# One fp32 product per chunk for two Gram matrices of a gated DeltaNet head

## The chip, the cores and the metric

The kernel runs on one core of one Trainium2 chip. The metric is the device time of one execution, in microseconds (us). Three runs of the kernel before gave 2437.64, 2440.42 and 2441.45 us; the median is 2440.42 us. One more execution was profiled; it took 2440.88 us, and the span of its trace is 2439.1 us. All rows below come from that execution.

## What is computed

The program is two decoder layers on a sequence of 1024 tokens with 1024 channels. Layer 0 mixes tokens with a gated DeltaNet of 8 heads of 128 channels, layer 1 with a causal convolution module; after each comes a squared-ReLU MLP. Only the DeltaNet matters here. Cut to what the change touches, it computes

```python
q, k, v = split(silu(causal_conv(h @ w_in)))          # q and k are then normalised per token
decay = exp(where(causal, gam[:, None] - gam[None, :], -inf))
a_kk  = where(strict, einsum('cd,sd->cs', k * beta, k) * decay, 0)   # first Gram matrix
t_inv = solve(eye + a_kk, eye)
a_qk  = einsum('cd,sd->cs', q, k) * decay                            # second Gram matrix
# scan over chunks: v_new = u - w @ state; o = q_dec @ state + a_qk @ v_new; state = ...
```

Both Gram matrices of a chunk have the keys as one operand. They are taken in fp32.

## The kernel before, in words

The sequence is cut into two halves of 512 tokens (`hf`), and a half into four chunks of 128 (`NC2`). A head of one half is a unit `u`, 0 to 15 (`u = 8*hf + h`). Keys, queries and values lie with channels on the partitions and 512 tokens side by side.

Three engines, TensorE, VectorE (DVE) and ScalarE (ACT), run in an order that is written out by hand. Each job is a generator; `add` gives each of its steps a due time, and at the end all steps are emitted in order of due time. Within these three engines instructions run in that order. GpSimdE (POOL) and the DMA queue of SyncE (SP) are ordered by the framework. Due times are in stages: unit `u` is projected in stage `u` or a little earlier, prepared from `u + 1` on (`head_prep`, times `PREP_AT`), its 16x16 diagonal blocks are inverted on GpSimdE (`head_sub`, at `u + 1 + 0.298`), the whole block by TensorE in stage `u + 2` (`head_inv`, first step at 0.0574, its first matmul at 0.2093), and the scan over the chunks runs in stage `u + 3` (`head_scan`, 24 steps from -0.063 to 0.8984; its matmuls on the state L632 and L645 to L649, its update of the state L655). `head_decay` makes E, the exponentials of the decay, at `u + 0.6769` to `u + 1.1256`.

What fills TensorE are the dense projections: each tile is 24 passes of 512 columns (L229 to L231), eight steps of three. `PLAN` says how many tiles a stage holds: projection tiles, tiles of the output gate z, and tiles of the output product; a stage without an entry has three projection tiles and, from stage 12 on, one z tile, which comes first. The tiles of a stage share it evenly: with n tiles, one lasts 1/n of a stage, and its eight steps are spread over that. Stage 7 has one tile more, for the gates of the second half; it comes first. After that tile, the gates pass through a chain of small steps (`token_gates`, times `G1_AT` after the tile's end; the reciprocal L354 and the GpSimdE steps L355 to L364 at 0.487, the matmuls L369 and L370 on `gcol` at 0.7341, exponentials on ScalarE at 0.7578). The weights of the next tile are split in two during a tile: `whi` on ScalarE at 0.4696 of the tile, `wlo` on VectorE (L396) at 0.6631.

`conv` takes a projected tile out of PSUM (ScalarE, L415 and L420, 0.04 after the tile's end), adds three taps on VectorE (L423), and applies SiLU (ScalarE, L426) at 0.3287 after the tile's end.

The 13 steps of `head_prep`, with their due times after `u + 1`, are: transposes of k (-0.0922); squares of it with their sums, and the addition of an epsilon on GpSimdE (-0.0063); the matmuls of the first Gram matrix, L483 (0.0109); the norms (0.0442); NT, the masked first matrix, L493, and the two DMAs that bring its diagonal blocks to GpSimdE's layout (0.1551); the scaled copies kd, L503 (0.1822); transposes of q (0.2501), squares of it (0.4031); transposes of v (0.7425) and their scaling (0.7828); the matmuls of the second Gram matrix, L526 (0.8401); its product with E, L528 (0.9083); q times its decay (1.542). Two PSUM banks, tag `pp`, serve all of it. Keys and queries have four buffers each.

Of the kernel before, what the change touches and what calls it, by code (L numbers as in the profile page):

```python
# [11 lines left out]
AF = mybir.ActivationFunctionType  # L12
ALU = mybir.AluOpType
# [7 lines left out]
HALF = 512  # L21
NH = 8
NCH = S // P
NC2 = NCH // 2
# [15 lines left out]
W_HI = 0.4696  # L40
W_LO = 0.6631
CONV_AT = (0.04, 0.0952, 0.1701, 0.2145, 0.3287)
PREP_AT = (-0.0922, -0.0063, 0.0109, 0.0442, 0.1551, 0.1822, 0.2501, 0.4031, 0.7425, 0.7828, 0.8401, 0.9083, 1.542)
DECAY_AT = (0.6769, 0.9619, 1.1256)
SUB_AT = 0.298
INV_AT = (
# [19 lines left out]
H0_AT = (0.8992, 1.98, 2.4218, 2.6956, 3.874, 4.2736, 6.2935, 6.8047)  # L66
G1_AT = (-0.0095, 0.088, 0.1601, 0.2135, 0.3241, 0.487, 0.7341, 0.7578, 1.2185, 1.3557)
PLAN = {
    0: (3, 0, ()), 1: (1, 4, ()), 2: (1, 2, ()), 3: (0, 2, ()), 4: (3, 0, ()), 5: (3, 0, ()), 7: (4, 0, ()), 8:
    (4, 0, ()), 14: (2, 1, ()), 15: (2, 1, ()), 16: (0, 2, ()), 17: (0, 2, (3,)), 18: (0, 0, (6, 0, 4, 7, 1)),  # L70
}


# [51 lines left out]
def tile_hybrid(ctx, tc, xT, c, adaT, cols, rows, gates, w_gate, w_first, w_dn, w_dno, w_cf, w_cfo,  # L125
                w_1, w_2, consts, out):
    nc = tc.nc
    ve, sc, te, gp = nc.vector, nc.scalar, nc.tensor, nc.gpsimd
    uid = [0]

    def nm(s):
        uid[0] += 1
        return f"{s}_{uid[0]}"
# [31 lines left out]
    def bank(tag):  # L165
        return banks["pool"].tile([P, HALF], F32, name=nm(tag), tag=tag, bufs=banks[tag])
# [3 lines left out]
    def blk(j):  # L170
        return slice(j * P, (j + 1) * P)
# [78 lines left out]
    def power(o, i, e):  # L250
        gp.tensor_tensor(o, i, expo[e][:, 0:i.shape[1]], op=ALU.pow)
# [49 lines left out]
        gp.memset(expo[e], e)  # L301


    db = Bufs("dn", pre=2, k=4, q=4, v=2, NT=2, A=2, Xc=2, o=2, gb=2, Rt=2, vt=2)
    VC = [P, NC2, P]
    GS = [P, NH, NC2]
    future = dp("future", P)
# [7 lines left out]
    beta, gam, negam, kdec, gdr = {}, {}, {}, {}, {}  # L315

    def v3(t):
        return t.rearrange("p (c m) -> p c m", m=P)

    def bc_col(t2d):  # L320
        return t2d.unsqueeze(2).broadcast_to(VC)
# [88 lines left out]
    def conv(d, nt, hf, tag, out):  # L410

        ps = d["ps"]
        pre = db("pre", HALF + CONV - 1)
        gp.tensor_copy(pre[:, 0:CONV - 1], hist[:, nt, :])
        sc.copy(pre[:, CONV - 1:], ps)  # L415
        if hf == 0:
            gp.tensor_copy(hist[:, nt, :], pre[:, HALF:])
        a = db(tag)
        b_ = C_CONV + nt * CONV
        sc.activation(a, ps, AF.Copy, scale=col[:, b_ + 3:b_ + 4])  # L420
        yield
        for j in range(3):
            ve.scalar_tensor_tensor(a, pre[:, j:j + HALF], col[:, b_ + j:b_ + j + 1], a,  # L423
                                    op0=ALU.mult, op1=ALU.add)
            yield
        sc.activation(a, a, AF.Silu)  # L426
        out[tag] = a
        yield
# [12 lines left out]
    def temp(kind, u):  # L441

        i = {"V": u % 2, "kd": 2 + u % 3, "E": 5 + u % 3}[kind]
        return hb(f"ax{i}_{1 if u < 10 else 0}")
# [19 lines left out]
    def head_prep(u, d):  # L464

        hf, h = divmod(u, NH)
        k = d["k"]

        kd = temp("kd", u)
        ssk, ssq = sm("ssk", NC2), sm("ssq", NC2)  # L470

        ps = bank("pp")
        for j in range(NC2):
            te.transpose(ps[:, blk(j)], k[:, blk(j)], ident)
        yield
        for j in range(NC2):
            sc.activation(kd[:, blk(j)], ps[:, blk(j)], AF.Square, accum_out=ssk[:, j:j + 1])
        gp.tensor_scalar(ssk, ssk, L2_EPS, None, op0=ALU.add)
        yield

        g = bank("pp")
        for j in range(NC2):
            te.matmul(g[:, blk(j)], lhsT=k[:, blk(j)], rhs=k[:, blk(j)], start=True, stop=True)  # L483
        yield
        nk = sm("nk", NC2)
        power(nk, ssk, 0.5)
        br2 = d["br2"] = sm("br2", NC2)
        ve.reciprocal(br2, ssk)
        ve.tensor_mul(br2, br2, beta[hf][:, h, :])
        yield  # L490
        NT = d["NT"] = db("NT")
        for j in range(NC2):
            ve.scalar_tensor_tensor(NT[:, blk(j)], g[:, blk(j)], br2[:, j:j + 1], d["E"][:, blk(j)],  # L493
                                    op0=ALU.mult, op1=ALU.mult)

        pitch = 8 * (NB * P + NB)
        d_in = dr.tile([NC2, pitch], F32, name=nm("d_in"), tag="d_in", bufs=2)
        nc.sync.dma_start(bass.AP(d_in.tensor, d_in.offset, [[P, P], [pitch, NC2], [1, P]]), v3(NT))
        A = d["A"] = db("A", [NB, NB], p=32)
        nc.sync.dma_start(A, bass.AP(d_in.tensor, d_in.offset, [[NB * P + NB, 32], [P, NB], [1, NB]]))  # L500
        yield
        for j in range(NC2):
            sc.activation(kd[:, blk(j)], ps[:, blk(j)], AF.Copy, scale=kdec[hf][:, h, j:j + 1])  # L503
        d["kd"] = kd
        yield
        ps = bank("pp")
        for j in range(NC2):
            te.transpose(ps[:, blk(j)], d["q"][:, blk(j)], ident)
        yield
        for j in range(NC2):  # L510
            sc.activation(ps[:, blk(j)], ps[:, blk(j)], AF.Square, accum_out=ssq[:, j:j + 1])
        gp.tensor_scalar(ssq, ssq, L2_EPS, None, op0=ALU.add)
        yield
        vn = hb("lo")
        ps = bank("pp")
        for j in range(NC2):
            te.transpose(ps[:, blk(j)], d["v"][:, blk(j)], ident)
        yield
        ve.tensor_tensor(v3(vn), v3(ps), bc_col(nk), op=ALU.mult)
        d["vn"] = vn  # L520
        eq = d["eq"] = sm("eq", NC2)
        ve.tensor_scalar(eq, ssq, RMS_EPS * P, None, op0=ALU.mult)
        yield
        g = bank("pp")
        for j in range(NC2):
            te.matmul(g[:, blk(j)], lhsT=k[:, blk(j)], rhs=d["q"][:, blk(j)], start=True, stop=True)  # L526
        yield
        ve.tensor_tensor(d["E"], g, d["E"], op=ALU.mult)  # L528
        d["kq"] = d["E"]
        yield  # L530

        ve.tensor_tensor(d["q"], d["q"], d["gb"], op=ALU.mult)
        d["qs"] = d["q"]
        yield
# [21 lines left out]
    def head_inv(u, d):  # L556

        NT = d["NT"]
        V, VT, W = temp("V", u), db("VT"), db("W")
# [16 lines left out]
        def at(t, j, r, c, n):  # L576
            return t[r:r + n, j * P + c:j * P + c + n]
# [3 lines left out]
        for j in range(NC2):  # L581
            te.matmul(ps[:, blk(j)], lhsT=NT[:, blk(j)], rhs=VT[:, blk(j)], start=True, stop=True)  # L582
        yield
# [9 lines left out]
        for b_, n in ((32, P), (64, 64)):  # L593
            yield from transposed(n)
            w = bank("pi")
            for j in range(NC2):
                for r in range(0, P, 2 * b_):
                    te.matmul(at(w, j, r + b_, r, b_), lhsT=at(NT, j, r, r + b_, b_), rhs=at(VT, j, r, r, b_),
                              start=True, stop=True)
# [163 lines left out]
    for u in range(2 * NH):  # L763
        n = f"{u // 8}{u % 8}"
        add("prep" + n, head_decay(u, heads[u]), *[max(u + p_, 0.98 + p_ / 100) for p_ in DECAY_AT])
        add("prep" + n, head_prep(u, heads[u]), *[u + 1 + p_ for p_ in PREP_AT])
        add("inv" + n, head_sub(u, heads[u]), u + 1 + SUB_AT)
# [488 lines left out]
```

## Time and profile before

| | |
|---|---|
| median of three runs | 2440.42 us (2437.64 to 2441.45) |
| the profiled execution, its time and its span | 2440.88 us, 2439.1 us |
| TensorE (PE) busy | 2378.8 us, 98% |
| VectorE (DVE) busy | 1724.6 us, 71% |
| ScalarE (ACT) busy | 1102.5 us, 45% |
| GpSimdE (POOL) busy | 419.5 us, 17% |
| chain that ended last, share of TensorE | 84% |

PE is TensorE's matmuls, PEld its weight loads, which run beside them. The stretch up to about 700 us holds the DeltaNet half of the work. In rows of the time order, the first number is the start in us after the span's start, the second the length; a bracket at the end gives how long the engine stood idle before the instruction and what released it. Matmuls overlap in the pipeline, so their spacing is read from one start to the next.

### The profile page before, as it was taken

Reading aid. Unit: us, or ns where it says so; the run is one execution under the profiler, and the core shown is the slowest. Engines: PE = TensorE matmul, PEld = TensorE weight load, DVE = VectorE, ACT = ScalarE, POOL = GpSimd, SP = SyncE. Lnnn points to the kernel's source line nnn. Section 1 sums busy time; section 2 is a strip of 40 time slices with the busy share of each in tenths; the row PEclk is TensorE's granted clock in tenths of the full one; section 3 lists DMA queues with packets and bytes.
Section 4 is the critical chain, followed back from the end, with each engine's and each line's share of the span. In section 5 each row is a group of like instructions: output and inputs, shape, how many; then the busy total and the mean of one; then the engine's idle time right before and its main releaser. Section 6 shows DMA issues by size and latency. Waiting matters only on the chain.

```text
span 2439.1 us, 31861 instructions
## 1 busy us (share of the span) xinstructions
PE 2378.8 (98%) x11962; PEld 1967.7 (81%) x11962; DVE 1724.6 (71%) x2634; ACT 1102.5 (45%) x1934; POOL 419.5 (17%) x903
## 2 busy tenths in 40 slices
PE   7889999999999999999999999999999999999998
PEld 6678888888777888888888888878888888888887
DVE  6656777676688664555899998899888766443447
ACT  4666776664346323333633334553333345333323
POOL 0546556455411000000000001100000001000003
PEclk9999999999999999999999999999999999999999
DMA  7342232333645654443223222323233232223223
GB/s 291 107 136 82 74 91 78 99 92 106 202 157 171 207 181 142 150 141 104 95 98 101 95 95 96 104 87 104 95 97 101 92 125 90 100 97 102 96 95 130
DMA packets 117994, 286.98 MB, mean 118 GB/s; under 512 B 35024, under 2 KB 44496, under 8 KB 117840
## 3 DMA queue, kind: packets, MB, share of 16 engines
q1 hardware_dynamic: 117840, 284.95, 36.0%
q8 instruction: 94, 1.54, 0.3%
q14 instruction: 60, 0.49, 0.1%
HBM read 275.40 MB, written 9.50 MB: 117 GB/s over the span
## 4 chain that ended last, share of the span: by engine, by line
PE 84%; DVE 7%; POOL 4%; DMA 3%; issue 1%; ACT 1%; SPq 0%; DVEq 0%; POOLq 0%; ACTq 0%
PE pd L229 25%; PE pd L231 25%; PE pd L230 25%; POOL X L546 1%; PE pp L943 1%; DVE wlo L396 1%; POOL T L544 1%; DMA raw<-in_adaT_dram 1%; DVE tl L994 1%; DVE tl L992 1%; DVE lo L241 1%; DVE raw L203 1%; DVE ax L254 1%; PE pi L582 1%; PE ps L645 1%
## 5 line engine op out<-in xcount | busy, mean ns | idle before, releaser
L229 PE MATMUL pd<-hh,whi 128*128 128x512 f32 x2016 | 820.0, 407 | 22.4 <-ACT whi L220 12.8
L231 PE MATMUL pd<-hh,wlo 128*128 128x512 f32 x2016 | 790.8, 393 | 2.3 <-DVE wlo L396 2.3
L230 PE MATMUL pd<-lo,whi 128*128 128x512 f32 x2016 | 789.6, 392 | 0.5 <-DVE lo L241 0.5
L393 ACT CAST whi<-raw 128x1024 fp32r<-128x1024 f32 x382 | 398.7, 1044 | 543.0 <-PE pd L230 518.0
L396 DVE TENSOR_TENSOR wlo<-raw,whi 128x1024 fp32r<-128x1024 f32 x382 | 466.9, 1223 | 19.5 <-ACT whi L393 17.8
L229 PEld LDWEIGHTS pd<-hh,whi 128*128 128x128 f32 x2016 | 381.6, 189 | 92.6 <-ACT whi L220 12.8
L231 PEld LDWEIGHTS pd<-hh,wlo 128*128 128x128 f32 x2016 | 380.3, 189 | 86.4 <-DVE wlo L396 4.0
L230 PEld LDWEIGHTS pd<-lo,whi 128*128 128x128 f32 x2016 | 382.1, 190 | 69.1 <-DVE lo L241 1.7
L229 PE MATMUL pd<-xh,whi 128*128 128x512 f32 (+1 forms) x1056 | 405.1, 384 | 1.3 <-DVE ax L254 1.3
L230 PE MATMUL pd<-xl,whi 128*128 128x512 f32 (+1 forms) x1056 | 404.1, 383 | 0.3 <-DVE xl L241 0.3
L231 PE MATMUL pd<-xh,wlo 128*128 128x512 f32 (+1 forms) x1056 | 404.1, 383 | 0.0
L922 DVE SCALAR_TENSOR_TENSOR cv<-u,col,cv 128x512 f32<-128x512 f32 x480 | 358.4, 748 | 9.6 <-ACT cv L918 1.8
L254 DVE SCALAR_TENSOR_TENSOR ax<-pd,mod,ax 128x512 f32<-128x512 f32 x280 | 207.8, 746 | 165.8 <-PE pd L231 164.8
L241 DVE TENSOR_TENSOR xl<-ts,xh 128x512 fp32r<-128x512 f32 x128 | 88.3, 690 | 245.8 <-ACT ts L866 245.3
L860 ACT ACTIVATE tz<-pd 128x512 f32<-128x512 f32 x128 | 76.5, 598 | 392.9 <-PE pd L231 392.9
L229 PEld LDWEIGHTS pd<-xh,whi 128*128 128x128 f32 x1056 | 198.5, 188 | 40.7 <-DVE ax L254 1.1
L230 PEld LDWEIGHTS pd<-xl,whi 128*128 128x128 f32 x1056 | 198.5, 188 | 39.1 <-DVE xl L241 0.5
L231 PEld LDWEIGHTS pd<-xh,wlo 128*128 128x128 f32 x1056 | 198.4, 188 | 38.8
L203 DVE CUSTOM_DVE_ANT_0 raw<-raw,condb 128x1024 f32<-128x1024 f32 x96 | 117.3, 1222 | 36.8 <-DMA raw<-in_adaT_dram 36.4
L952 POOL TENSOR_SCALAR lnst<-mv 128x1 f32<-128x1 f32 x32 | 16.2, 506 | 530.7 <-DVE mv L951 360.7
L546 POOL TENSOR_TENSOR X<-X,T 32x15 f32<-32x15 f32 (+7 forms) x240 | 98.0, 408 | 18.7
L544 POOL TENSOR_TENSOR T<-X,A 32x15 f32<-32x15 f32 (+7 forms) x240 | 84.1, 350 | 27.2 <-DMA A<-d_in 9.4
(215 smaller groups left out, 2246.1 us busy)
## 6 DMA issues: line engine op xcount, KB each, us to landing
raw<-in_w_dram SPq DMA_DIRECT2D x260, 512.0 KB, 3.6
raw<-in_adaT_dram SPq DMA_DIRECT2D x96, 512.0 KB, 3.9
raw<-in_w_dn_dram SPq DMA_DIRECT2D x57, 512.0 KB, 4.0
raw<-in_w_cf_dram SPq DMA_DIRECT2D x32, 512.0 KB, 3.8
raw<-in_w_dno_dram SPq DMA_DIRECT2D x16, 512.0 KB, 3.7
raw<-in_w_cfo_dram SPq DMA_DIRECT2D x16, 512.0 KB, 3.7
tz<-in_xT_dram SPq DMA_DIRECT2D x16, 256.0 KB, 7.8
raw<-in_w_first_dram SPq DMA_DIRECT2D x8, 512.0 KB
```

The source lines that it names most:

```text
L203: ve.tensor_tensor_reduce(out=raw, in0=raw, in1=condb, op0=ALU.mult, op1=ALU.add, scale=1.0, scalar=0.0, accum_out=mod[l][j][:, k:k + 1])
L229: te.matmul(ps, lhsT=w[0][:, s_], rhs=ah, start=(first and i == 0), stop=False)
L230: te.matmul(ps, lhsT=w[0][:, s_], rhs=al, start=False, stop=False)
L231: te.matmul(ps, lhsT=w[1][:, s_], rhs=ah, start=False, stop=(last and i == n - 1))
L241: ve.tensor_tensor(lo, x32, hi.bitcast(F32), op=ALU.subtract)
L254: ve.scalar_tensor_tensor(AX[hf][k], ps, g[:, k:k + 1], AX[hf][k], op0=ALU.mult, op1=ALU.add)
L393: sc.copy(hi, raw)
L396: ve.tensor_tensor(lo, raw, hi.bitcast(F32), op=ALU.subtract)
L544: gp.tensor_tensor(t, X[:, 0:i + 1, i:i + 1].broadcast_to(sh), A[:, i:i + 1, i + 1:].broadcast_to(sh), op=ALU.mult)
L546: gp.tensor_tensor(X[:, 0:i + 1, i + 1:], X[:, 0:i + 1, i + 1:], t, op=ALU.subtract)
L860: sc.activation(r, d[0], AF.Relu)
L922: ve.scalar_tensor_tensor(cv, u[:, j:j + HALF], col[:, b_ + j:b_ + j + 1], cv, op0=ALU.mult, op1=ALU.add)
```

## The change

Keys and queries of a unit become the two halves of one tile (`pair`), so that one matmul with a chunk's keys as weights and 256 columns, the chunk's keys and then its queries, gives both Gram matrices. Two chunks fill a PSUM bank; `gram(0)` and `gram(1)` fill two. The copies kd move ahead of the matmuls, the norms too; the product of the second matrix with E becomes two instructions and moves up behind NT and its DMAs. Due times are changed accordingly: 11 steps, the norms at 0.0442, the two Gram steps at 0.085 and 0.11, NT and the product with E at 0.1551, the rest as before. Keys and queries have four paired buffers. Four entries of `PLAN` go: stages 7 and 8 have three projection tiles in place of four (stage 7 with the gate tile besides), and stages 14 and 15 have three in place of two, with one z tile as before.

```diff
-PREP_AT = (-0.0922, -0.0063, 0.0109, 0.0442, 0.1551, 0.1822, 0.2501, 0.4031, 0.7425, 0.7828, 0.8401, 0.9083, 1.542)
+PREP_AT = (-0.0922, -0.0063, 0.0442, 0.085, 0.11, 0.1551, 0.2501, 0.4031, 0.7425, 0.7828, 1.542)
...
-    0: (3, 0, ()), 1: (1, 4, ()), 2: (1, 2, ()), 3: (0, 2, ()), 4: (3, 0, ()), 5: (3, 0, ()), 7: (4, 0, ()), 8:
-    (4, 0, ()), 14: (2, 1, ()), 15: (2, 1, ()), 16: (0, 2, ()), 17: (0, 2, (3,)), 18: (0, 0, (6, 0, 4, 7, 1)),
+    0: (3, 0, ()), 1: (1, 4, ()), 2: (1, 2, ()), 3: (0, 2, ()), 4: (3, 0, ()), 5: (3, 0, ()), 16: (0, 2, ()), 17: (0, 2, (3,)), 18: (0, 0, (6, 0, 4, 7, 1)),
...
-    db = Bufs("dn", pre=2, k=4, q=4, v=2, NT=2, A=2, Xc=2, o=2, gb=2, Rt=2, vt=2)
+    db = Bufs("dn", pre=2, kq=4, v=2, NT=2, A=2, Xc=2, o=2, gb=2, Rt=2, vt=2)
...
-        a = db(tag)
+        if tag == "v":
+            a = db(tag)
+        else:
+
+            if "pair" not in out:
+                out["pair"] = db("kq", [2, HALF])
+            a = out["pair"][:, 0 if tag == "k" else 1]
...
-        yield
-
-        g = bank("pp")
         for j in range(NC2):
-            te.matmul(g[:, blk(j)], lhsT=k[:, blk(j)], rhs=k[:, blk(j)], start=True, stop=True)
-        yield
+            sc.activation(kd[:, blk(j)], ps[:, blk(j)], AF.Copy, scale=kdec[hf][:, h, j:j + 1])
+        d["kd"] = kd
+        yield
+
+
+        def gram(i):
+            g = bank("pp").rearrange("p (c t m) -> p c t m", c=2, t=2)
+            for j in range(2):
+                c_ = blk(i * 2 + j)
+                te.matmul(g[:, j], lhsT=k[:, c_], rhs=d["pair"][:, :, c_], start=True, stop=True)
+            return g
+
...
+        g = [gram(0)]
+        yield
+        g.append(gram(1))
+        yield
         NT = d["NT"] = db("NT")
         for j in range(NC2):
-            ve.scalar_tensor_tensor(NT[:, blk(j)], g[:, blk(j)], br2[:, j:j + 1], d["E"][:, blk(j)],
+            ve.scalar_tensor_tensor(NT[:, blk(j)], g[j // 2][:, j % 2, 0], br2[:, j:j + 1], d["E"][:, blk(j)],
...
-        yield
-        for j in range(NC2):
-            sc.activation(kd[:, blk(j)], ps[:, blk(j)], AF.Copy, scale=kdec[hf][:, h, j:j + 1])
-        d["kd"] = kd
+        E = v3(d["E"])
+        for i in range(2):
+            ve.tensor_tensor(E[:, i * 2:i * 2 + 2], g[i][:, :, 1], E[:, i * 2:i * 2 + 2], op=ALU.mult)
+        d["kq"] = d["E"]
...
-        yield
-        g = bank("pp")
-        for j in range(NC2):
-            te.matmul(g[:, blk(j)], lhsT=k[:, blk(j)], rhs=d["q"][:, blk(j)], start=True, stop=True)
-        yield
-        ve.tensor_tensor(d["E"], g, d["E"], op=ALU.mult)
-        d["kq"] = d["E"]
```

## Rows read from the trace of the kernel before

**Rows 1.** The page's first part: an engine's busy time, share of span, instructions.

```profile
PE 2378.8 (98%) x11962; PEld 1967.7 (81%) x11962; DVE 1724.6 (71%) x2634; ACT 1102.5 (45%) x1934; POOL 419.5 (17%) x903
```

**Rows 2.** What TensorE waited for, 0 to 900 us: total, times, longest.

```profile
PE pp L369 <- POOL gcol L364: 5.3, 2, 4.0
PE ps L645 <- DVE vt L641: 4.9, 3, 2.3
PE pi L582 <- DVE VT L562: 4.4, 1, 4.4
```

**Rows 3.** TensorE's groups, whole span, shapes apart: weights, columns; busy us, mean ns; idle.

```profile
L483 PE MATMUL pp<-k 128*128 128x128 f32 x128 | 16.8, 274 | 0.0
L979 PE MATMUL pp<-ident,lnst 128*8 128x128 f32 x8 | 2.2, 272 | 4.7 <-POOL lnst L954 4.7
L369 PE MATMUL pp<-gcol,kcl 128*128 128x32 f32 x4 | 0.8, 286 | 5.3 <-POOL gcol L364 5.3
```

**Rows 4.** TensorE in order of time: head 0's first Gram matrix; then 256-column passes.

```profile
91.55 1.05 PE L483 MATMUL pp<-k 128*128 128x128 f32 x8
...
92.68 0.39 PE L230 MATMUL pd<-lo,whi 128*128 128x512 f32 x1
92.91 0.40 PE L231 MATMUL pd<-hh,wlo 128*128 128x512 f32 x1
...
2411.00 0.28 PE L229 MATMUL pd<-xh,whi 128*128 128x256 f32 x1
2411.12 0.28 PE L230 MATMUL pd<-xl,whi 128*128 128x256 f32 x1
```

**Rows 5.** Groups of VectorE and ScalarE, 0 to 900 us.

```profile
L528 DVE TENSOR_TENSOR ax<-pp,ax 128x512 f32<-128x512 f32 x16 | 11.0, 685 | 7.7 <-PE pp L526 7.7
L503 ACT ACTIVATE ax<-pp,kdec 128x128 f32<-128x128 f32 x64 | 18.1, 363 | 0.0
```

**Rows 6.** ScalarE, VectorE and TensorE in order of time, start of stage 12.

```profile
444.32 0.63 ACT L457 ACTIVATE ax<-ax 128x512 f32<-128x512 f32 x1
445.38 1.12 ACT L503 ACTIVATE ax<-pp,kdec 128x128 f32<-128x128 f32 x4
...
444.98 1.13 DVE L493 SCALAR_TENSOR_TENSOR NT<-pp,br,ax 128x128 f32<-128x128 f32 x4 [0.64 <-ACT ax L457]
...
447.82 0.34 DVE L655 SCALAR_TENSOR_TENSOR S<-S,gl,ps 128x128 f32<-128x128 f32 x1
...
449.29 0.39 PE L632 MATMUL ps<-S,k 128*128 128x128 f32 x2
```

**Rows 7.** Head 0: E's exponential, NT, and TensorE's wait for its inverse.

```profile
95.34 0.63 ACT L457 ACTIVATE ax<-ax 128x512 f32<-128x512 f32 x1
...
96.30 1.12 DVE L493 SCALAR_TENSOR_TENSOR NT<-pp,br,ax 128x128 f32<-128x128 f32 x4
...
130.99 1.47 PE L582 MATMUL pi<-VT,NT 128*128 128x128 f32 x8 [4.43 <-DVE VT L562]
```

**Rows 8.** Stage 7: the gate chain on GpSimdE, and TensorE's wait for its end.

```profile
300.30 0.29 POOL L352 TENSOR_SCALAR gz<-gy 128x32 f32<-128x32 f32 x1
...
312.94 0.24 POOL L364 TENSOR_TENSOR gcol<-gq,nea 128x32 f32<-128x32 f32 x1
...
313.23 0.41 PE L369 MATMUL pp<-gcol,kcl 128*128 128x32 f32 x2 [1.25 <-POOL gcol L364]
```

**Rows 9.** Busy us of PE, PEld, DVE, ACT, POOL; granted clock; DMA share, GB/s.

```profile
120.00:140.00 20.00, 15.57 (x78) 12.99 (x77) 12.70 (x26) 12.52 (x31) 6.38 (x15) 0.91 0.61 188
300.00:320.00 20.00, 18.57 (x112) 14.64 (x111) 13.23 (x28) 13.74 (x33) 12.06 (x36) 1.00 0.34 99
```

**Rows 10.** Stages 16 and 17: ScalarE and TensorE in order of time.

```profile
571.93 0.70 ACT L420 ACTIVATE v<-pd,col 128x512 f32<-128x512 f32 x1
...
572.79 0.38 PE L638 MATMUL ps<-Rt,ax 128*128 128x128 f32 x2
...
601.81 0.49 PE L645 MATMUL ps<-vt,ax 128*128 128x128 f32 x2 [2.35 <-DVE vt L641]
```

More of the change, by code (lines that the diff above doesn't have):

```diff
@@ L478, in head_prep @@
         gp.tensor_scalar(ssk, ssk, L2_EPS, None, op0=ALU.add)
+        for j in range(NC2):
+            sc.activation(kd[:, blk(j)], ps[:, blk(j)], AF.Copy, scale=kdec[hf][:, h, j:j + 1])
+        d["kd"] = kd
         yield
-        g = bank("pp")
-        for j in range(NC2):
-            te.matmul(g[:, blk(j)], lhsT=k[:, blk(j)], rhs=k[:, blk(j)], start=True, stop=True)
-        yield
+        def gram(i):
[4 more added lines that the diff above has]
+            return g
         nk = sm("nk", NC2)
@@ L522, in head_prep @@
         ve.tensor_scalar(eq, ssq, RMS_EPS * P, None, op0=ALU.mult)
-        yield
-        g = bank("pp")
-        for j in range(NC2):
-            te.matmul(g[:, blk(j)], lhsT=k[:, blk(j)], rhs=d["q"][:, blk(j)], start=True, stop=True)
-        yield
-        ve.tensor_tensor(d["E"], g, d["E"], op=ALU.mult)
-        d["kq"] = d["E"]
         yield
```

## The prediction, made before the change was run

> **What bounds the kernel now.** The page first: TensorE is busy 98% of the span [rows 1], so the time changes only if TensorE gets less work, or if it stands still more or less than today. Next, the waits of TensorE in the stretch that holds the DeltaNet half (0 to 900 us): they are few, and each has a place [rows 2]. In the stages 1 to 16 that the change touches they are the two waits for the gate columns (L369, 5.3 us in all; the second, in stage 7, is 1.25 us [rows 8]), one wait of 4.4 us for head 0's inverse (L582), and 4.9 us in three waits of the scan (L645). Steady stages have practically none: there VectorE, ScalarE, GpSimdE and the SP queue run beside TensorE with some slack. So I price TensorE's own instructions first, and then ask at each boundary whether a moved step uses up that slack.
>
> **TensorE's instructions.** An fp32 product is two instructions here (L483: 128 for 64 products [rows 3]). Eight of them, head 0's first Gram matrix, take from 91.55 to 92.68 less the one 512-column pass in between (0.23): 0.90 us, 0.1125 each [rows 4]. Both matrices of a head: 16 halves, 1.80 us. After the change: 8 halves of 256 columns. No row shows an fp32 half of more than 128 columns, so two bounds. Lower: it streams one column per cycle as the 256-column fp32r pass does, 0.12 us [rows 4]; 0.96 us a head, 13.4 us saved over 16 heads. Upper: two cycles a column, as a 512-column pass, 0.23 us [rows 4]; 1.84 us a head, +0.6 us in all. What sets today's 0.1125, the columns or the weight load? L979 moves 128 columns against 8 weight columns and takes 272 ns, as long as L483 with 128 (274): columns. L369 moves 32 columns against 128 weight columns and takes 286: weights too [rows 3]. Both sides cost the same in a square product, so halving the loads saves nothing unless columns are cheaper than L979 says. I take the upper bound, **+0.6 us**; VectorE and SP cannot hide it either way.
>
> The Trainium skill (TensorE: Matmul & The Clock Gate, "LDWEIGHTS (loading the stationary operand)") has a weight load cost its columns at 1.2 GHz, an estimate of 107 ns for 128: by that rule alone the load would be today's limit and the lower bound would come within reach. Its page FP8 and Floating Point Precision ("TensorE Precision Notes") counts four passes for true fp32, which over two instructions is the upper bound. No row separates them; the first is the first rival below.
>
> **Work that is merely moved.** Four scaled copies of kd (L503, 363 ns each [rows 5], 1.1 us) go from behind the exponentials of E to ahead of them on ScalarE. At the boundary of stage 12, E's exponential is done at 444.95 and VectorE's first NT step starts at 444.98 [rows 6]: there ScalarE is the later one, so NT moves by 1.1 us. Behind NT come the two new products with E; today's single one is 685 ns [rows 5], so two halves cost between 0.7 and 1.4 us; I take 0.85. What is queued behind on VectorE (taps of the convolution, wlo, the state update L655) comes 1.9 us later. The state update ended at 448.16 and TensorE took it up at 449.29 [rows 6]: 1.1 us of slack, plus 0.9 because TensorE now does the second Gram matrix before that point. It just holds: cost nought, and if it does not, some 0.3 us at each such head. The d_in transfer behind NT shifts SP's queue by the same 1.1 us, and weight loads behind it are issued about a tile before use, which covers that. Gram matrices now hold both pp banks until the products with E are done; q's transposes come at slot 0.2501, three us after NT's slot: hidden. The pair buffer waits for the scan of head u-4, which ends at u-0.10, half a stage ahead of k's copy at u+0.37: hidden. The product with E, and its matmul, vanish from slots 0.84 and 0.91: nobody was held there.
>
> **Early stages.** Head 0's NT starts at 96.30, E's exponential ends at 95.97 [rows 7]: with 1.1 us more, NT moves by 0.8, and so does the chain through d_in, substitution and d_out to the 4.43 us wait at 130.99. But TensorE meanwhile does head 1's second matrix inside that wait (0.9 us that it need not do later). Net -0.1; where W of the inverse (behind the new products) comes late, up to +1.0. I take **+0.3**.
>
> **The plan: stage 7.** Stages 7 and 8 lose a tile each, 14 and 15 gain one. Work is conserved, but the gate columns are a chain on GpSimdE. It ends at 313.18, after the substitution of head 6 is done (300.30) and 26 small steps; TensorE waited from 311.98 [rows 8]. In the new plan the gate tile ends at 7.25 instead of 7.2, so L369 lands at slot 7.984: TensorE has one tile less to do ahead of it (24 passes of 0.23, 5.5 us) and two more of the last tile's eight steps (1.4 us): it arrives at about 307.7. GpSimdE's chain starts about 1 us earlier, since one wlo step (1.2 us) leaves the place before NT; it ends near 312.1. The wait grows from 1.25 to 4.4: **+3.1 us** (bounds +1 and +5). A 4.43 us wait at 131 went with a granted clock of 0.91 over its 20 us, that is 1.2 GHz for 3.6 of them; the 1.25 us wait did not (1.00) [rows 9]. At half speed 3.6 us do the work of 1.8: **+1.7 us**. Head 7's first product of both matrices also waits, for q's SiLU (below), but within that slow stretch: nought more.
>
> **The new wait on q.** Until now the matrix with q ran at u+1.84. Now TensorE needs q at u+1.085, in order, so all projections queue behind it. In a stage with four tiles q is the third; its SiLU stands at u+1.0787. At heads 12 to 14 TensorE has three tile steps and one scan product (2.3 us) before it, which covers copies and SiLU: **+0.5 us** for all such boundaries together (0 to 1.5). At head 15 stage 16 has only two long tiles: one tile step, L638 (572.79 today, 0.9 earlier without the old matrix), then the product, at 572.1. ScalarE's copy of v ends at 572.63 [rows 10]; add 1.1 for kd, and q's SiLU, now behind that copy rather than ahead of it: 573.75. A wait of 1.65 us. The next wait, the 2.3 us one [rows 2] near 601, hangs on head 15's own chain and is shortened by what TensorE lost; that chain moves by 1. Net **+0.5** (-1 to +3).
>
> **Sum.** 0.6 + 0.3 + 3.1 + 1.7 + 0.5 + 0.5 = 6.7 us on the profiled execution of 2440.88 us (span 2439.1): 2447.6. The median of the three runs is 0.46 below it, so 2447.1; I say 2447.
>
> **Rivals.** (1) Columns are cheap (the lower bound): 14 us less than my sum, 2433, faster. For it: L369's 286 ns; against: L979's 272. It decides as soon as a 256-column half takes under 0.16 us. Chance 0.15. (2) The waits are hidden: GpSimdE begins the gate chain before it finishes other steps, and q is ready: only +0.6 remains, 2441. For it: in the substitution GpSimdE already lets other small steps in; against: 26 serial steps cannot be shortened. Chance 0.25. (3) Stage 8, one tile shorter, no longer covers head 7's substitution, and TensorE also waits for its inverse in stage 9, 3 us and another spell at 1.2 GHz: 2452. Against: NT to the inverse has about 6 us of room. Chance 0.08. The forecast itself, 0.52.
>
> **How the numbers follow.** A measurement of this kernel tells 0.2% (4.9 us) from no change. Of the forecast's 0.52, three quarters lie beyond +4.9 (0.39), with rival 3: slower 0.47. The other quarter and rival 2: same 0.38. Rival 1: faster 0.15. Range: 2436 to 2454; it leaves out rival 1 and a tail above, and takes in the bounds of the stage 7 wait and of the tail.
>
> **What would show it.** L483's successors: a mean pitch of 0.23 (or 0.12). TensorE's wait for gcol in stage 7: over 4 us, with a clock below 1.00 in those 20 us. A wait of about 1.7 us for q's SiLU at stage 16. NT a microsecond later than today in stages after a three-tile stage, and no wait at L632 from it. If the gate wait stays near 1 us, the step on the plan is wrong; if TensorE's busy time falls by over 10 us, the step on columns is.

## The result and the profile after

The changed kernel takes 2458.53 us (median of 4 runs, 2456.39 to 2459.39) against 2440.44 for the kernel before beside it (4 runs): a ratio of 1.0075, 95% interval 1.0057 to 1.0092. It is 18 us slower. The forecast, 2447, had the direction; the time lies above the range (2436 to 2454). The profiled execution took 2456.39 us with a span of 2454.6, 15.5 us more than the span before.

The page's first line for TensorE, to set beside [rows 1]:

```profile
PE 2384.2 (97%) x11834; PEld 1967.4 (80%) x11834; DVE 1726.7 (70%) x2650; ACT 1106.7 (45%) x1936; POOL 421.2 (17%) x903
```

There are 128 instructions fewer on TensorE and 5.4 us more busy time. The projections are the same and the Gram products take no longer (below), so I looked at the waits and at the granted clock next. First TensorE's waits in the changed kernel between 290 and 400 us (total, times, longest):

```profile
PE ps L654 <- DVE vt L650: 4.5, 1, 4.5
PE pp L368 <- POOL gcol L363: 4.1, 1, 4.1
PE pi L597 <- DVE W L593: 0.6, 1, 0.6
PE pp L494 <- ACT kq L431: 0.3, 1, 0.3
```

That is 9.5 us; before, the same stretch held the gate wait of 1.3 [rows 2, 8] and 0.2 more. (vt is a short step on VectorE between two products of the scan, W one between two products of the inverse.) Then stretches of 20 us (busy us of TensorE, its instructions, granted clock, DMA share, GB/s), three of the changed kernel and two of the kernel before:

```profile
300.00:320.00 20.00, 15.63 (x76) 0.83 0.33 99
340.00:360.00 20.00, 15.52 (x89) 0.92 0.27 74
360.00:380.00 20.00, 20.00 (x141) 0.91 0.19 56
...
340.00:360.00 20.00, 20.00 (x127) 1.00 0.30 88
360.00:380.00 20.00, 20.00 (x157) 1.00 0.29 77
```

Before, all three stood at 1.00 (the first is in [rows 9]). The clock has two levels here, 2.4 and 1.2 GHz, and the figure is its mean over the stretch. What the clock takes is read straight from this: 20 x (1 - 0.83) = 3.4 us in the first, 20 x (0.08 + 0.09) = 3.4 in the other two. So 290 to 400 us alone holds 8.0 us of new waits and 6.8 of clock, 14.8 of the 15.5 us. The rest of the kernel nearly balances: from 100 to 290 us TensorE waits 1.5 us longer, but a stretch at 1.2 GHz that stood near 160 us is gone.

**The wait in stage 7.** The end of the gate chain on GpSimdE, and TensorE in order of time behind it, in the changed kernel:

```profile
312.25 0.24 POOL L363 TENSOR_TENSOR gcol<-gq,nea 128x32 f32<-128x32 f32 x1
...
312.54 0.63 PE L368 MATMUL pp<-gcol,kcl 128*128 128x32 f32 x2 [4.10 <-POOL gcol L363]
...
313.99 0.63 PE L229 MATMUL pd<-lo,whi 128*128 128x512 f32 x1
314.41 0.63 PE L230 MATMUL pd<-hh,wlo 128*128 128x512 f32 x1
```

The chain ends 0.7 us earlier than before [rows 8], but TensorE is there 4.1 us ahead of it. Behind the wait a 512-column pass takes 0.42 us from start to start, where it takes 0.23 in [rows 4]: that is the lower clock in the single rows.

**The wait in stage 9.** In the changed kernel, VectorE and TensorE first, then SP's queue (issue of each transfer), and the longest wait of that queue from 330 to 360 us:

```profile
335.39 0.27 DVE L381 COPY grow<-pp 32x128 f32<-32x128 f32 x1
...
346.22 0.34 DVE L664 SCALAR_TENSOR_TENSOR S<-S,gl,ps 128x128 f32<-128x128 f32 x1
354.92 1.14 DVE L459 SCALAR_TENSOR_TENSOR ax<-gb,gam,future 128x128 f32<-128x128 f32 x4 [8.36 <-DMA gb<-gdr]
...
356.86 0.69 DVE L571 TENSOR_TENSOR VT<-Xc,kcl 128x512 f32<-128x512 f32 x1
357.46 0.35 DVE L650 TENSOR_SCALAR vt<-ps,br 128x128 f32<-128x128 f32 x1
...
357.87 0.80 PE L654 MATMUL ps<-vt,ax 128*128 128x128 f32 x2 [4.48 <-DVE vt L650]
```

```profile
344.63 0.32 SPq L559 DMA_DIRECT2D d_out<-X  x1
346.33 0.37 SPq L562 DMA_DIRECT2D Xc<-d_out  x1
346.81 0.50 SPq L190 DMA_DIRECT2D raw<-in_w_dn_dram  x1
347.38 0.42 SPq L383 DMA_DIRECT2D gdr<-grow  x1
350.85 0.33 SPq L455 DMA_DIRECT2D gb<-gdr  x1
...
SPq L559 <- POOL X L556: 17.4, 1, 17.4
```

And the same place in the kernel before, SP's queue and VectorE:

```profile
344.49 0.33 SPq L550 DMA_DIRECT2D d_out<-X  x1
344.92 0.36 SPq L384 DMA_DIRECT2D gdr<-grow  x1
346.13 0.38 SPq L553 DMA_DIRECT2D Xc<-d_out  x1
346.61 0.53 SPq L450 DMA_DIRECT2D gb<-gdr  x1
```

```profile
351.06 1.14 DVE L454 SCALAR_TENSOR_TENSOR ax<-gb,gam,future 128x128 f32<-128x128 f32 x4 [1.14 <-DMA gb<-gdr]
```

Read it from the end. TensorE waits for vt; vt is a short step on VectorE, and VectorE had stood for 8.4 us at another step, the decay matrix of head 8, which needs the broadcast gb of the second half's decay rows. The rows themselves (grow) were on the chip at 335.7, but SP issues in order, and its queue stood behind d_out, which waits for head 7's substitution. Now the write of the rows goes behind Xc and a weight load too, at 347.4 rather than 344.9, and the broadcast at 350.9 rather than 346.6. VectorE had waited 1.1 us here before: there was no slack at all. Its wait grew by 7.2 us from two sides: the step on gb starts 3.9 us later (354.9 for 351.1), and VectorE, with a tile less ahead of it, is there 3.4 us earlier (346.6 for 349.9). The substitution itself is not later: d_out goes out at 344.6, before at 344.5.

**The Gram products.** TensorE in order of time, head 1 in the changed kernel:

```profile
123.27 1.03 PE L494 MATMUL pp<-kq 128*128 128x256 f32 x4
123.94 0.59 PE L228 MATMUL pd<-hh,whi 128*128 128x512 f32 x1
124.37 0.40 PE L229 MATMUL pd<-lo,whi 128*128 128x512 f32 x1
```

From the first half to the second pass behind the group: 1.10 us. In [rows 4] the same distance, with eight halves of 128 columns, is 1.13. Take off the one pass (0.23) and a half of 256 columns costs 0.22 us, twice the 0.1125 of a half of 128. The change's title operation saves 0.02 to 0.03 us in each of 32 groups, by estimate about 1 us in all.

### The profile page after: what moved, and what is told of

It reads as the page before. It is cut to its first block, busy times and chain, and to the rows that moved or that the text cites. A ratio compares the mean times of both kernels' runs of the same rounds, so it can differ in the third digit from the quotient of the medians.

```text
span 2454.6 us, 31618 instructions
## 1 busy us (share of the span) xinstructions
PE 2384.2 (97%) x11834; PEld 1967.4 (80%) x11834; DVE 1726.7 (70%) x2650; ACT 1106.7 (45%) x1936; POOL 421.2 (17%) x903
## 4 chain that ended last, share of the span: by engine, by line
PE 81%; DVE 8%; POOL 5%; DMA 3%; issue 1%; ACT 1%; SPq 0%; DVEq 0%; POOLq 0%; ACTq 0%
PE pd L228 24%; PE pd L230 24%; PE pd L229 24%; POOL X L555 2%; POOL T L553 2%; PE pp L952 1%; DVE wlo L395 1%; DVE tl L1001 1%; DVE tl L1003 1%; DVE lo L240 1%; DMA raw<-in_adaT_dram 1%; DVE ax L253 1%; PE pp L494 1%; DVE raw L202 1%; DMA d_out<-X 0%
## 5 line engine op out<-in xcount | busy, mean ns | idle before, releaser
L553 POOL TENSOR_TENSOR T<-X,A 32x15 f32<-32x15 f32 (+7 forms) x240 | 89.7, 374 | 23.9 <-DMA A<-d_in 6.5
```

Source lines behind the costliest of these rows:

```text
L553: gp.tensor_tensor(t, X[:, 0:i + 1, i:i + 1].broadcast_to(sh), A[:, i:i + 1, i + 1:].broadcast_to(sh), op=ALU.mult)
```

## The experiments

Theory: the plan (one tile fewer in stages 7 and 8) uncovers two waits, for the gate columns and, by way of SP's queue, for gb. Rival A: the moved steps (kd ahead, both matrices together, products with E behind NT) cost the time. Rival B: the wide product does. All ratios are to the kernel before, run beside each (its medians 2439.8 to 2441.0).

**The old plan, the moved steps.** From the changed kernel:

```
-    db = Bufs("dn", pre=2, kq=4, ...
+    db = Bufs("dn", pre=2, k=4, q=4, ...
...
+    ... 7: (4, 0, ()), 8: (4, 0, ()), 14: (2, 1, ()), 15: (2, 1, ()), ...
...
-                te.matmul(g[:, j], lhsT=k[:, c_], rhs=d["pair"][:, :, c_], start=True, stop=True)
+                for t, b in enumerate((k, d["q"])):
+                    te.matmul(g[:, j, t], lhsT=k[:, c_], rhs=b[:, c_], start=True, stop=True)
```

> The changed kernel, but with the plan of tiles of before (stage 7 and 8 four tiles each, 14 and 15 two and one), and, since that plan needs a fifth pair tile that has no room, with keys and queries in separate tiles and two products of 128 columns where the change has one of 256. Everything else that the change moves (both matrices together, the products with E behind NT, the copies of kd ahead) stays. Theory (the plan of stages 7 and 8 made the loss): the waits of 4.1 us (gate columns) and 4.5 us (stage 9) go back to 1.3 and nought, the granted clock is 1.00 in 300 to 320 us and in 360 to 380 us, and the time is 2441 to 2445 us. Rival A (the moved steps made it): 2455 or more, with the waits still there. Rival B (the wide product itself costs): also 2441 to 2445, but then the next kernel, which has the new plan alone, stays at 2441.

Measured: 2448.66 us, 1.0038 (1.0026 to 1.0050), 8.8 us above the kernel before beside it: between the theory and rival A. The wait in stage 9 is gone (the write of the decay rows goes out straight behind d_out again, ahead of Xc, and VectorE waits 2.0 us for gb); the gate wait is not back at 1.3, but at 2.4, and a stretch at 1.2 GHz follows it. Waits from 290 to 400 us, and stretches:

```profile
PE pp L369 <- POOL gcol L364: 2.4, 1, 2.4
...
300.00:320.00 20.00, 17.64 (x106) 0.89 0.35 99
320.00:340.00 20.00, 20.00 (x113) 0.94 0.22 68
```

**The new plan alone**, in the kernel before:

```
-    ... 7: (4, 0, ()), 8: (4, 0, ()), 14: (2, 1, ()), 15: (2, 1, ()), 16: ...
+    ... 16: ...
```

> The kernel before with one edit: the four entries of the plan are dropped (stages 7 and 8 three tiles, 14 and 15 as the rest), its Gram products and all its steps as they were. Theory (plan): 2453 to 2459 us, with a wait of over 3 us for the gate columns near 311 us, a wait of about 4 us in stage 9, and a clock near 0.83 and 0.92 in the 20 us around each. Rival A (moved steps) or B (wide product): 2441 to 2443, no new wait.

Measured: 2456.23 us, 1.0069 (1.0056 to 1.0082). As the theory had it: the plan alone costs 16 us, where the whole change costs 18. TensorE's long waits of that run, in order of time:

```profile
312.03 0.64 PE L368 MATMUL pp<-gcol,kcl 128*128 128x32 f32 x2 [4.66 <-POOL gcol L363]
...
357.12 0.49 PE L644 MATMUL ps<-vt,ax 128*128 128x128 f32 x2 [2.84 <-DVE vt L640]
```

The stage 9 wait was shorter than expected (2.8 for 4), and there was a third in between, 2.2 us for W at 326.8. Plan (16) and moved steps (9) add up to more than the 18 of both: both lengthen the same gate wait (2.4 by the steps, 4.7 by the plan, 4.1 together) and its slow stretch is paid once. That last is argued from the waits, not tested.

**The decay rows by another queue.** From the changed kernel:

```
-        nc.sync.dma_start(d.rearrange("h (c p) -> (h c) p", p=P), grow)
+        (nc.scalar if hf else nc.sync).dma_start(d.rearrange("h (c p) -> (h c) p", p=P), grow)
...
-        nc.sync.dma_start(gb, gdr[hf][h:h + 1, :].broadcast_to([P, HALF]))
+        (nc.scalar if u == NH else nc.sync).dma_start(gb, gdr[hf][h:h + 1, :].broadcast_to([P, HALF]))
```

> The changed kernel; the write of the second half's decay rows and the broadcast of them for head 8 go out from ScalarE's DMA queue, not from SP's, where they stood behind the transfers that wait for head 7's substitution. Theory (VectorE's step on gb is what delays vt and so TensorE in stage 9): the 8.4 us wait of VectorE for gb falls under 2 us, TensorE's wait of 4.5 us near 358 and the stretch at half clock behind it go, the gate wait stays: 2458.5 - 4.5 - 3.4 = 2450.6 us (2449 to 2453). Rival (head 7's own substitution or the inverse is late, as my prediction had it): the wait stays within 1 us of 4.5, under another name, and the time within 2 us of 2458.

Measured: 2452.72 us, 1.0056 (1.0043 to 1.0070). The wait for vt and its slow stretch are gone, and VectorE no longer waits for gb:

```profile
337.78 0.36 ACTq L383 DMA_DIRECT2D gdr<-grow  x1
...
340.95 0.35 ACTq L455 DMA_DIRECT2D gb<-gdr  x1
...
348.92 1.13 DVE L459 SCALAR_TENSOR_TENSOR ax<-gb,gam,future 128x128 f32<-128x128 f32 x4
```

TensorE's program was as in the changed kernel, and head 7's substitution ended no earlier: d_out went out at 346.4, there at 344.6. So the stage 9 wait was gb behind SP's queue. In 290 to 400 us the profile gives back the 7.9 us expected (waits 9.5 to 5.0, clock 6.8 to 3.4); the medians give 5.8.

**The gate products later.** From the changed kernel:

```
-G1_AT = (..., 0.487, 0.7341, 0.7578, 1.2185, 1.3557)
+G1_AT = (..., 0.487, 0.95, 0.97, 1.2185, 1.3557)
```

> The changed kernel; the two products on the gate columns and what reads them are due at 7.95 and 7.97 in place of 7.7341 and 7.7578, so TensorE has the rest of the last tile ahead of them (three passes of one k-tile later by the order, behind which it used to wait). Theory (GpSimdE's chain ends at 312.25 whatever TensorE does): a step that is due only some 0.7 us later shortens the wait of 4.1 us by 0.7 and no more, so this edit gives 0.7 us unless the wait falls to where the clock is not taken back (the wait of 3.3 us at 131 us still went with 3.4 us at half clock, the one of 2.65 us at 159.5 us did not): 2455 to 2458.5. Rival (the wait itself is not on the path that sets the end, since the wait in stage 9 would swallow it): within 1 us of 2458.5 even if the wait falls by more.

Measured: 2454.0 us (2448.39 to 2455.86), 1.0055 (1.0042 to 1.0068), below what I gave. I had misread how far the edit moves the products: not by 0.7 us, but behind both Gram halves of head 7, so TensorE comes to them at 319.0 in place of 308.4. By then the columns are there; what L368 waits for is the pp bank that the products with E still read. That wait is 2.0 us with no stretch at 1.2 GHz behind it; the stage 9 wait stays at 3.9 with its slow stretch. The rival (the gate wait is swallowed by the next) is out. Waits from 290 to 400 us:

```profile
PE ps L654 <- DVE vt L650: 4.3, 2, 3.9
PE pp L368 <- DVE ax L519: 2.0, 1, 2.0
```

**Both edits.**

> The changed kernel with both edits: the second half's decay rows from ScalarE's DMA queue, and the two products on the gate columns due at 7.95 and 7.97. Theory (two separate waits, each with its own stretch at 1.2 GHz): the savings add. Singly they were 5.8 and 4.5 us on the medians, and 7.9 and 6.2 us in the stretch 290 to 400 us of the profiled runs, so 2444 to 2449 us, with less than 3 us of TensorE idle in 290 to 400 us and no stretch at 1.2 GHz there. Rival (one wait moves into the next): 2451 or more.

Measured: 2447.7 us (2443.38 to 2454.76), 1.0030 (1.0018 to 1.0042): 10.8 us below the changed kernel, where the two singly gave 4.5 and 5.8. The savings add, within the spread of these runs. Waits from 290 to 400 us are 2.2 in all; of the clock 1.8 us are still lost there, which I had not expected:

```profile
PE pp L368 <- DVE ax L519: 1.9, 1, 1.9
...
320.00:340.00 20.00, 20.00 (x145) 0.94 0.18 46
```

**One tile moved back**, to stage 7 or to stage 8. From the changed kernel, with the entries of one of these lines put into `PLAN`:

```
+    ... 7: (4, 0, ()), 14: (2, 1, ()), ...
...
+    ... 8: (4, 0, ()), 14: (2, 1, ()), ...
```

> The changed kernel, pairs and wide product as they are, with one tile moved back: stage 7 has four tiles again (and stage 14 two and one), stage 8 stays at three. Theory: the gate wait falls from 4.1 to some 2.4 us (as in the run with the old plan), the wait in stage 9 stays at 3 to 4.5 us with its stretch at 1.2 GHz, since stage 8 is what covers it: 2453 to 2457 us. Rival (stage 7's length sets both, since the whole frame moves with it): both waits go, 2448 or less.

> The changed kernel with the other tile moved back: stage 8 has four tiles again (and stage 14 two and one), stage 7 stays at three. Theory: the gate wait stays at 4 us with 6.8 us at 1.2 GHz behind it, the wait in stage 9 goes: 2450 to 2453 us, as where the decay rows went by ScalarE's queue (2452.7). Rival: the wait in stage 9 stays and the time is above 2456.

Measured: 2453.27 (1.0055, 1.0042 to 1.0067) and 2455.12 (1.0057, 1.0045 to 1.0070). The first came in the time expected, with a gate wait of 2.4; the wait for vt in stage 9 was 2.0, shorter than the 3 to 4.5 given, and there was one of 1.2 for the state update S ahead of it. The second missed: the gate wait stays at 4.1 with 6.8 us at 1.2 GHz, the wait for vt falls to 1.4 but does not go, and the time is some 2 us over the expectation. VectorE still waits for gb, 6.1 us in the first and 5.2 in the second, and in both the decay rows are written behind Xc: a tile in either stage only covers a part of SP's delay.

**The old plan with the gate products later** (the edit of G1_AT in the old-plan kernel).

> The run with the old plan (moved steps, separate tiles, products of 128 columns: 2448.7 us), with the products on the gate columns due at 7.95 and 7.97. Theory (what the moved steps cost with the old plan comes mostly through the gate wait, which they raise from 1.3 to 2.4 us, over the point where a stretch at 1.2 GHz follows): the wait falls under 1 us, the stretch goes, 2448.7 - 2.0 - 3.3 = 2443.4 us (2441.5 to 2445.5). Rival (the moved steps cost it in many small waits of the scan and the inverse): 2447 or more.

Measured: 2452.15 us (2447.61 to 2454.94), 1.0044 (1.0031 to 1.0057). My theory failed. The gate wait did fall to 0.85 and the clock from 300 to 400 us is 1.00 throughout, but the time did not fall; the intervals of this run and of the old-plan run overlap, so no difference between them is shown. Nor did the waits of 290 to 400 us: they are 3.4 us in both, since a new wait of 1.1 us for vt and longer ones for W took the place. Here too the write of the decay rows had slipped behind Xc (issued at 349.1), and VectorE waited 4.6 us for gb, where it waited 2.0 in the old-plan run. With the plan as before, the gate wait is not where the moved steps' cost can be got back.

**The products with E later**, in the old-plan kernel (a step boundary ahead of them, due at 0.28, with q's transposes at 0.33):

```
-PREP_AT = (..., 0.11, 0.1551, 0.2501, 0.4031, ...
+PREP_AT = (..., 0.11, 0.1551, 0.28, 0.33, 0.4031, ...
...
+        yield
         E = v3(d["E"])
```

> The run with the old plan (moved steps, separate tiles: 2448.7 us), with the two products with E put behind the step W of the inverse and the state update S of the scan on VectorE, in place of straight behind NT; q's transposes, which need the bank, follow them. Theory (what the moved steps cost is VectorE's time ahead of W and S): TensorE's waits for W and S, 1.6 and 2.0 us in 100 to 660 us with the old plan against 0.5 and 0.6 before, fall by 2 us or more, the sum of its waits there goes from 17.9 to 15 us or less, and the time is 2444 to 2446.5 us. Rival (the copies of kd ahead of E's exponential are the cost): waits and time within 1.5 us of 2448.7.

Measured: 2460.84 us, 1.0090 (1.0076 to 1.0104): 12 us the other way. TensorE's waits from 100 to 660 us rose from 17.9 to 27.0 us; the two longest groups:

```profile
PE ps L644 <- DVE br L496: 6.2, 4, 2.7
PE pp L521 <- DVE ax L516: 5.8, 8, 1.1
```

L521 are q's transposes: they need a pp bank, and both are held by the two Gram halves until the products with E are done. That is 5.8 us of new waits; the first row, in the scan, had 1.8 with the old plan, and why it grew is not shown. The experiment did not isolate VectorE's time; it showed what putting the products off costs once both matrices sit in both banks.

**The copies of kd ahead, alone**, in the kernel before (the four copies moved up behind the squares, their slot 0.1822 dropped).

> The kernel before with one edit: the four scaled copies of kd go ahead of the exponential of E, as the change has them. Theory by my prediction's row (ScalarE is the later one ahead of NT, so NT and the whole chain to the gate columns move by 1.1 us): the gate wait rises from 1.3 to about 2.4 us, and at that length a stretch at 1.2 GHz follows (as with the old plan): 2440.5 + 1.1 + 3.4 = 2445 us (2443 to 2447). Rival (the products with E behind NT are what costs, the copies are covered): 2439 to 2442, gate wait under 1.6 us.

Measured: 2442.04 us (11 runs), 1.0009 (1.0000 to 1.0018), 2.2 us, with nought at the edge of the interval. The gate wait is 1.2 and no slow stretch follows. As far as the gate wait goes the rival is right and I was not: one microsecond more on ScalarE ahead of the exponential of E doesn't reach the gate chain. The trace of before has a reason, at head 6, whose substitution the chain follows:

```profile
275.97 0.63 ACT L457 ACTIVATE ax<-ax 128x512 f32<-128x512 f32 x1
...
279.12 1.12 DVE L493 SCALAR_TENSOR_TENSOR NT<-pp,br,ax 128x128 f32<-128x128 f32 x4
```

The exponential is done at 276.6 and NT starts 2.5 us later, as VectorE is busy until then: here VectorE is the later one, not ScalarE as in [rows 6].

**Everything that helped, together** (four tiles in stage 7, gate products later, decay rows from ScalarE's queue).

> The changed kernel with all that helped it singly: stage 7 at four tiles (stage 14 two and one), the products on the gate columns due at 7.95 and 7.97, the second half's decay rows from ScalarE's DMA queue. Theory (waits add): no wait over 2 us and no stretch at 1.2 GHz in 290 to 400 us; with the moved steps' own 3 to 6 us left: 2443 to 2447 us, a little below the kernel with the last two edits (2447.7), still above the kernel before. Rival (the pairs are at least free once the plan is right): 2441 or less.

Measured: 2449.14 us, 1.0043 (1.0029 to 1.0057), above the 2443 to 2447 that I gave and not below the 2447.7 of the two edits. The waits don't simply add: a new one of 4.6 us came up. VectorE and TensorE in order of time:

```profile
336.11 0.75 DVE L679 TENSOR_TENSOR o<-o,ss 128x512 f32<-128x512 f32 x1 [5.17 <-POOL ss L250]
...
338.25 0.34 DVE L664 SCALAR_TENSOR_TENSOR S<-S,gl,ps 128x128 f32<-128x128 f32 x1
...
338.65 0.79 PE L641 MATMUL ps<-S,kq 128*128 128x128 f32 x2 [4.58 <-DVE S L664]
```

It has the same form as the one in stage 9: TensorE waits for a third of a microsecond on VectorE, which stands behind a step that waits for another engine.

**Two products of 128 columns for one of 256**, in the changed kernel:

```
-                te.matmul(g[:, j], lhsT=k[:, c_], rhs=d["pair"][:, :, c_], start=True, stop=True)
+                for t in range(2):
+                    te.matmul(g[:, j, t], lhsT=k[:, c_], rhs=d["pair"][:, t, c_], start=True, stop=True)
```

> The changed kernel with one edit: each wide product of 256 columns is made as two products of 128 columns, from the same pair tile into the same places. All steps stand where the change has them. Theory (two cycles a column, the wide product gives nothing but its few boundaries): a half of 128 columns has a pitch near 0.112 us, one of 256 has 0.2155, so 256 x 0.112 - 128 x 0.2155 = 1.1 us more of TensorE, and a time within 2 us of the changed kernel's 2458.5. Rival (a wide product is markedly cheaper than two): 2465 or more.

Measured: 2462.56 us, 1.0087 (1.0073 to 1.0101), 4 us above the changed kernel, more than the bound of 2 (the two intervals overlap). The pitch itself is as expected:

```profile
123.22 1.05 PE L495 MATMUL pp<-kq 128*128 128x128 f32 x8
124.03 0.48 PE L228 MATMUL pd<-hh,whi 128*128 128x512 f32 x1
124.35 0.39 PE L229 MATMUL pd<-lo,whi 128*128 128x512 f32 x1
```

1.13 us from the first half to the second pass, against 1.10. The other 3 us are in longer waits (gate 5.6, vt in stage 9 5.6); why these grew is not shown. Rival B (the wide product costs) is out: without it the kernel is no faster.

**The products with E left out**, in the old-plan kernel, in the kernel before and in the changed kernel. The edits take out the lines with `ve.tensor_tensor(... op=ALU.mult)` that multiply E by the Gram matrix.

> The run with the old plan (moved steps, separate tiles: 2448.7 us), with the two products with E on VectorE left out (the output's part within a chunk then lacks the keys times queries; nothing waits for them). Theory (VectorE's 1.4 us behind NT, ahead of W, S and the taps, is what the moved steps cost): 2440.5 to 2444 us, that is the 2442.0 of the copies of kd alone, and TensorE's waits in 100 to 660 us for vt, W, S and br, together 11.6 us with the old plan, fall to 8 or less. Rival (TensorE's order and the pp banks): 2446 or more, the waits within 1.5 us of 11.6.

> The kernel before with its one product with E per head (685 ns on VectorE at slot 0.9083) left out: the same part of the output is missing. It is the price of that step where it stood. Theory (it stood in slack): 2438 to 2442, that is no change. Rival (VectorE is short everywhere, wherever the step stands): 2436 or less.

> The changed kernel with the two products with E left out (the same part of the output is missing). Theory (VectorE's time behind NT): 2450 to 2455 us: the plan's own waits for the gate columns (4 us) and in stage 9 (3 to 4.5 us) stay, each with its stretch at 1.2 GHz, the small waits for W, S and br go. Rival (TensorE's order): 2456 to 2460, as the changed kernel.

Measured: 2448.11 (1.0034, 1.0022 to 1.0047), 2440.44 (1.0002, 0.9993 to 1.0011) and 2456.01 (1.0070, 1.0058 to 1.0083): 0.6, nothing and 2.5 us less than with them. In the first, TensorE's waits for vt, W, S and br are 10.3 us, where 8 or less was expected and 11.6 was the old plan's: the rival's account. The third falls just inside the rival's range, and its waits for the gate columns and in stage 9 stay (4.8 and 4.3 us). VectorE's time for the products is not what the moved steps cost with the old plan. What that kernel still waits for there, 290 to 400 us:

```profile
PE pp L369 <- POOL gcol L364: 2.7, 1, 2.7
PE ps L634 <- DVE S L657: 1.6, 1, 1.6
PE pi L590 <- DVE W L586: 0.5, 1, 0.5
```

So of the 8.8 us of the moved steps with the old plan, the kd copies take some 2 and VectorE's products up to 1. The other 6 are what is left when these are taken off, a difference of medians that differ by 2 us and less; no run isolates them. What else moved is the matrices with q, now at the stage's start, the first Gram matrices, now behind the norms, and the hold on both pp banks. In the old-plan run TensorE's waits from 100 to 660 us are 17.9 us against 11.7 before, and all of them are for short steps on VectorE and for the gate columns, none for a bank. Which of the moves it is stays open.

## Why the prediction was wrong, step by step

- **Columns.** The choice of the upper bound was right: 0.22 us a half, not 0.12. Its argument (L979 against L483) was weak: the mean lengths, 272 to 286 ns for 32 to 128 columns, are over twice the spacing of 0.1125 us, and L369 with a quarter of the columns is no shorter; they do not tell what sets the spacing. That the choice came out by this argument is partly luck; the spacing of the 256-column halves decides it. It was costed at +0.6 us and measured at about -1. Half as many loads, and twice the time for each half: halving the loads did not pay, and rival 1 is out. The Trainium skill (TensorE: Matmul & The Clock Gate, "LDWEIGHTS (loading the stationary operand)") has a load cost its columns at 1.2 GHz, an estimate of 107 ns for 128; the 0.1125 us of a half of 128 columns lie too near that to tell load from columns, the 0.22 us of a half of 256 do not.
- **Stage 7, the wait.** Predicted: TensorE there at 307.7, chain's end at 312.1, wait 4.4, +3.1. Measured: 308.4, 312.25, 4.1, +2.8. This step held to within a microsecond in each of its times.
- **Stage 7, the clock.** The term was mis-sized: +1.7, from the 4.4 us wait of head 0 with its 0.91 [rows 9]. The new wait, nearly as long, was followed by 0.83, which is 3.4 us. One row is no price for the clock: waits of like length had one or the other.
- **Stage 9.** Here the prediction failed: the step that followed SP's queue. It was in the forecast at nought and stood as rival 3 at 0.08, with 3 us and a spell: 2452. It came with 4.5 us and 3.4 of clock, 7.9 in all, which is most of the 11.5 us between forecast and time. Rival 3 had the place, and half of the cause: SP's queue did stand for head 7's substitution. But TensorE did not wait for the inverse; "NT to the inverse has about 6 us of room" looked at head 7's inverse, and that one was not late. The prediction asked of SP's queue only whether weight loads come late. I had followed the gate step's products on TensorE into their new slot, and not the write of the decay rows that it issues, nor the broadcast that head 8's decay step issues behind it: they go through SP's queue behind d_out, and VectorE waits for them in order, ahead of vt. With both sent by ScalarE's queue the wait and its stretch were gone, and the time fell by 5.8 us. The row that would have said so was in the trace of before: VectorE already waited 1.14 us for gb.
- **Work that is merely moved.** "It just holds: cost nought" was about right for VectorE's products (0.6 to 2.5 us by leaving them out) and for the kd copies (2.2 us). NT did move where ScalarE is the later one: from the squares of k to NT, heads 9 to 11 took 4.8, 5.0 and 5.8 us before and 5.7, 5.7 and 6.7 in the changed kernel. At head 6, ahead of the gate chain, it did not. "It just holds" was a little short: TensorE's waits for the state update S rose from 0.6 to 1.9 us, and for W from 0.5 to 1.8 (100 to 660 us). And "nobody was held" does not cover the matrices with q at the stage's start: with the old plan about 6 us are left over once the rest is taken off, and there is no term for them. The step on the banks was right only because the products come straight behind NT; put off, they made TensorE wait 5.8 us for a bank, in a kernel that was 12 us longer.
- **The early stages, the wait on q, the tail.** Between 100 and 290 us +1.5 of waits and -1.8 of clock, for +0.3. The wait for q's SiLU at stage 16 was 0.94 us where 1.65 was worked out; there was another of 0.28 in stage 8, none at the other boundaries. The wait behind it was 2.44 for 2.35 [rows 10] and not shortened. Small terms, and near enough.

By the profiled runs: -1 (columns), -0.3 (early), +2.8 and +3.4 (stage 7), +4.5 and +3.4 (stage 9), +0.7 (other waits from 290 to 400 us), +0.4 (waits from 400 to 740 us) is 13.9 of 15.5 us; 1.6 are not placed. Each of these terms is read from one execution, and the clock varies from one to the next: the stretch at 120 to 140 us stands at 0.91 in both kernels here, at 0.83 in the run of the kernel before without its product with E, which was no slower. The "gate wait over 4 us with a clock below 1.00", which was to show the forecast right, was there; what the list of signs lacked was a look at stage 9.

No version here beats the kernel before. The change saves about 1 us of TensorE, and comes with a plan that costs 16. The two go together only in part: under the whole plan of before, four pair tiles are one too few and a fifth has no room beside the kernel's other buffers, so no run has both; but with four, stage 7 or stage 8 alone can have its fourth tile back, at 2453.3 and 2455.1 us.

## What to carry to other kernels

When a step is moved, follow every transfer that it issues through its queue, and ask which engine waits for the landing and what stands behind that wait in order. Two of TensorE's long waits here, 4.5 and 4.6 us, were for steps of 0.3 us on VectorE, which had itself been held up by something else; look at what that engine waited for, not at the step. A row that says which engine is the later one holds for its own head only: ScalarE was it in stage 12, VectorE ahead of the gate chain. And where TensorE is busy 98% of the span, a new wait must be priced with the clock behind it: in the changed kernel each of the two cost its own length and 3.4 us more.

## What the runs showed of the hardware

The stretches at 1.2 GHz did not grow smoothly with the wait. The 20 us around the waits of 1.25 us [rows 8, 9] and 1.4 us (the run with four tiles in stage 8) show 1.00. The gate wait was 2.35 us both with the old plan and with four tiles in stage 7: in the one 0.89 and 0.94 follow, (2.2 + 1.2) us lost, in the other 0.91 alone, 1.8 us lost. The waits of 4.1 and 4.5 us lost 3.4 each. The wait of 5.6 us in stage 9 with two products of 128 columns was followed by one stretch at 0.91, 1.8 us lost; the one of 4.6 us in the last combination by 0.82 and 0.92, 5.2 lost. Two equally long waits can thus cost a different number of microseconds, and a saving of a wait by half may or may not bring its clock back. What decides between them, the runs don't show.
